# Output projection's entry: three weight tiles move from SyncE's DMA queue to ScalarE's

## The chip, the cores and the metric

The kernel runs on one core of a Trainium2 chip. A core has five engines that run their own instruction streams: TensorE (PE in the profile, with its weight loads as PEld), VectorE (DVE), ScalarE (ACT), GpSimd (POOL) and SyncE (SP). SP computes nothing here; it issues most of the DMA transfers. ACT and POOL can issue transfers too, and a transfer that ACT issues stands in ACT's instruction stream, between its activations. The metric is the device time of one execution in microseconds (us), as the median of several runs.

## The reference

One inference step of a hybrid decoder layer, in float32, for a prompt of 1024 tokens and for 8 sequences of 8 new tokens each, with a paged cache of 8192 past positions. Cut to its core:

```python
n = rmsnorm(h, g_mix);  u = n @ w_in                    # one input projection
o_gla = gated linear attention (4 heads, chunked, exact recurrence)
o_mla = latent attention (8 heads; the sampled tokens attend over the paged cache:
        per page: kv = ckv @ w_kvup, rms-normed keys, running softmax)
h = h + concat([o_gla, o_mla]) @ w_o                    # output projection, 1024 x 1024
y, conv_new = conv_ffn(rmsnorm(h, g_ffn), conv_prev)    # 1024 -> 2816 -> 1024, width-3 conv
h = h + y
h = h + (p @ ple_w_proj) * sigmoid(rmsnorm(h, g_ple) @ ple_w_gate)
```

The outputs are h for prompt and samples, the new cache rows, and the new states.

## The kernel before

Every float32 product is made of pairs: `split` (L113 to L117) casts a tile to a rounded high part on ACT (L115) and subtracts it on DVE for the low part (L116), and a product is three matmuls, high by high, high by low, low by high (L139 to L141; in the output projection L1432, L1435 and L1436).

The work has two streams. The *dense* stream is the prompt's: input projection, gated linear attention, prompt attention. The *cache* stream is the samples' attention over 64 blocks of cached pages. A cache block gathers its pages (craw and krraw, by POOL's indirect DMA), transposes them (ctp, L522), splits them (cTh, cTl), and multiplies them by the key weights (ks, L139 to L141), whose squares ACT takes (csq, L560) and DVE sums (css, L565). DVE and POOL make the norms and the scores from that (ca and cy at L588 to L590, sn at L592 and L594, the block's maximum ml at L598 and L599, which PE transposes at L616 as mt). ACT takes the exponential (L628), and PE the product with the values (cpv, L645). The rotary part of the keys goes through crp (L500), kTh and kTl, and csr.

A loop at the end of `dense` hands out cache steps by a table of due times while there is dense work. When the dense stream ends, at about 1060 us, the generator `wo_units` takes its place: units of the prompt's output projection are then placed between the remaining cache blocks. The order of the instructions on each engine is set by a scheduler, which simulates the program when it is built; on each engine they run in that order.

The output projection's inner dimension is cut into chunks of 128 rows; a group has two chunks, and a group's work has four quarters (half the prompt's tokens by half the output's columns). For a unit `wo_unit` (L1422) multiplies the two chunks' attention rows (`sh`, `sl`) by the chunks' weights (`wh`, `wl`) into one bank ps_dn, and DVE adds it to the row block of h (L1439). Four kinds of raw data come in:

- `wo_rows(c, n)` (L1403) loads 256 KB of attention output of chunk c (oraw, from a scratch in DRAM) and splits it.
- `wo_cols(c, f)` (L1413) loads 256 KB of the weight w_o of chunk c and column half f (wraw) and splits it into wdh and wdl.
- `hrows(t)` (L1550) is the tile of the prompt's rows t, eight of them of 512 KB each, into which x_prompt is loaded.
- `conv_state` (L1478) loads the convolution's weights (cvec) and state (sc), which PE transposes (pt_cv, pt_sc).

oraw, wraw, cvec and sc share one ring of three buffers (`stage`, L1395): the fourth load waits until the first buffer's subtraction is done. At the first group's first quarter the loads are issued in this order on SP: two oraw and the first wraw (these three stand early, while the dense stream still runs), four rows h0 to h3, the second chunk's wraw, row h4, the two wraw of the other column half, rows h5 to h7, and the rows of x_sample. Each DMA also has one of a few completion semaphores, which it shares with an earlier transfer, and it waits until that one has landed.

Of the kernel before, what the change touches and what calls it, by code (L numbers as in the profile page):

```python
# [18 lines left out]
P = 128  # L19
# [25 lines left out]
def step_kernel(ctx: ExitStack, tc: tile.TileContext, A):  # L45
    nc = tc.nc
    pe, act, dve, pool, sp = nc.tensor, nc.scalar, nc.vector, nc.gpsimd, nc.sync
# [1348 lines left out]
    def stage(shape, dt, name):  # L1396
        return z["sg"].tile(shape, dt, tag="stage", name=name, bufs=3)
# [7 lines left out]
    def wo_rows(c, n):  # L1405

        hl = [z["wf"].tile([P, 512], F32R, tag=f"s{n}{k}", name=f"s{k}", bufs=2) for k in "hl"]
        raw = stage([P, 512], F32, "oraw")
        sp.dma_start(raw, doT[c * P:(c + 1) * P, n * 512:n * 512 + 512])
        split(*hl, raw)  # L1410
        wos[c, n] = hl

    def wo_cols(c, f):  # L1413

        hl = [z["wq"].tile([P, 512], F32R, tag=f"wd{f}{k}", name=f"wd{k}", bufs=2) for k in "hl"]
        raw = stage([P, 512], F32, "wraw")
        sp.dma_start(raw, A["w_o"][0][c * P:(c + 1) * P, f * 512:f * 512 + 512])
        split(*hl, raw)
        wow[c, f] = hl

    def hrows(t):
        return z["hs"] if t == NT else z["h"][t] if isinstance(z["h"], dict) else z["h"][:, t, :]  # L1422
# [113 lines left out]
    def wo_units():  # L1536

        for g in range(3):  # L1540
            grp = (2 * g, 2 * g + 1)
            f0 = g % 2
            quarters = ((0, f0), (0, 1 - f0), (1, 1 - f0), (1, f0))
            for q, (n, f) in enumerate(quarters):
                if g == 0 and q == 0:
                    for ld, x in ((wo_rows, 0), (wo_cols, 0)):
                        for c in grp:
                            ld(c, x)
                    for t in range(NT):
                        sp.dma_start(hrows(t), A["x_prompt"][0, t * P:(t + 1) * P, :])  # L1550
                        if t == 3:
                            for ld, x in ((wo_cols, 1), (wo_rows, 1)):
                                for c in grp:
                                    ld(c, x)
                    sp.dma_start(z["hs"], A["x_sample"].rearrange("b t d -> (b t) d"))
                    yield
                for t in range(4 * n, 4 * n + 4):
                    wo_unit(grp, t, f)
                    if q == 2 and t == 4 and g < 2:
                        for e in range(2):  # L1560
                            down_sample([(oTg[:, c], wow[c, e]) for c in grp], pd, e)
                    yield
                nx = (grp[0] + 2, grp[1] + 2)
                for c in nx:
                    if q == 1:
                        wo_rows(c, 0)
                    elif q == 2:
                        wo_cols(c, 1 - f0)
                    elif q == 3:
                        wo_cols(c, f0)  # L1570
                        wo_rows(c, 1)
            if g == 0:
                conv_state()
                gain("g_ffn")
                sp.dma_start(z["WvT"].rearrange("p (h c) -> p h c", h=8),
                             A["mla_w_kvup"][0].rearrange("p (h c) -> p h c", c=P)[:, :, 64:128])
        for t in order:
            for f in range(2):
                wo_unit((6, 7), t, f)
                if f:  # L1580
                    normed(t)
                yield
# [103 lines left out]
    ring = [0]  # L1686
# [569 lines left out]
```

## Time and profile before

| | us |
|---|---|
| median of 3 runs | 2216.89 |
| lowest and highest run | 2215.88, 2218.55 |
| the profiled execution's own time | 2221.39 |
| its span in the profile | 2219.6 |
| mean granted TensorE clock in it | 0.984 of full speed |
| the stretch from the end of the dense stream to the last unit of the first quarter | about 1060 to 1089 |

In the rows below, L1417 is line 1417 of the kernel before; out<-in names the tiles, xcount the number of instructions, and a bracket at the end of a row is the time that the engine stood idle before it, and what ended that idle time. "SPq" and "ACTq" are the DMA issues of SP and ACT: their time is that of the issue, not of the transfer. An engine's granted clock (PEclk) is 1.00 at full speed. Rows of a timeline begin with the start in us and the length.

### The profile page before, as it was taken

Reading aid. Unit: us, or ns where it says so; the run is one execution under the profiler, and the core shown is the slowest. Engines: PE = TensorE matmul, PEld = TensorE weight load, DVE = VectorE, ACT = ScalarE, POOL = GpSimd, SP = SyncE. Lnnn points to the kernel's source line nnn. Section 1 sums busy time; section 2 is a strip of 40 time slices with the busy share of each in tenths; the row PEclk is TensorE's granted clock in tenths of the full one; section 3 lists DMA queues with packets and bytes.
Section 4 is the critical chain, followed back from the end, with each engine's and each line's share of the span. In section 5 each row is a group of like instructions: output and inputs, shape, how many; then the busy total and the mean of one; then the engine's idle time right before and its main releaser. Section 6 shows DMA issues by size and latency. Waiting matters only on the chain.

```text
span 2219.6 us, 38384 instructions
## 1 busy us (share of the span) xinstructions
PE 2134.6 (96%) x13460; PEld 1934.7 (87%) x13460; DVE 1666.6 (75%) x2551; ACT 1369.1 (62%) x3726; POOL 1227.5 (55%) x1330
## 2 busy tenths in 40 slices
PE   7999999999999999999999987999999999999999
PEld 6888978878888888887788876999999999888899
DVE  4775676467788888887888878888888886887642
ACT  5576766777778888887777766433333433534631
POOL 5675668576777777777445557666656562011100
PEclk9899999999999999999999998999999999999999
DMA  5343234412342222221521212322232325778321
GB/s 181 110 141 110 77 117 157 141 54 69 104 120 60 64 73 61 60 56 46 167 80 57 76 66 96 105 92 95 91 100 91 100 87 190 238 222 237 98 72 41
DMA packets 204418, 233.07 MB, mean 105 GB/s; under 512 B 42422, under 2 KB 146339, under 8 KB 204227
## 3 DMA queue, kind: packets, MB, share of 16 engines
q1 hardware_dynamic: 188259, 179.49, 25.8%
q0 software_dynamic: 14736, 46.67, 7.3%
q10 hardware_dynamic: 1232, 4.46, 0.5%
q8 instruction: 108, 1.77, 0.3%
q14 instruction: 83, 0.68, 0.1%
HBM read 188.00 MB, written 42.52 MB: 104 GB/s over the span
## 4 chain that ended last, share of the span: by engine, by line
PE 80%; DVE 7%; ACT 5%; DMA 4%; POOL 2%; issue 2%; SPq 0%; DVEq 0%; POOLq 0%; ACTq 0%
PE ps_gu L140 7%; PE ps_gu L141 7%; PE ps_gu L139 7%; PE ks L139 5%; PE ks L141 5%; PE ks L140 4%; PE ps_dn L141 3%; PE ps_dn L140 3%; PE ps_dn L139 3%; PE cpv L645 2%; PE ctp L522 2%; PE ps_lt L278 2%; PE ps_pj L139 2%; PE ps_pj L140 1%; PE ps_pj L141 1%
## 5 line engine op out<-in xcount | busy, mean ns | idle before, releaser
L560 ACT ACTIVATE csq<-ks 128x256 f32<-128x256 f32 x1040 | 392.2, 400 | 88.1 <-PE ks L141 78.0
L565 DVE TENSOR_REDUCE css<-csq 128x16 f32<-128x1024 f32 (+1 forms) x264 | 315.8, 1197 | 63.0 <-ACT csq L560 61.9
L115 ACT CAST wh<-st 128x512 fp32r<-128x512 f32 x176 | 108.4, 619 | 188.6 <-PE ps_gu L140 166.0
L139 PE MATMUL ks<-mv0h,cTh 128*128 128x320 f32 (+1 forms) x520 | 171.9, 333 | 6.9 <-ACT csq L560 3.0
L139 PE MATMUL ks<-mv1h,cTh 128*128 128x320 f32 (+1 forms) x520 | 170.4, 329 | 7.6 <-ACT sn L562 3.6
L604 POOL TENSOR_TENSOR chl<-craw,chl 128x1024 fp32r<-128x1024 f32 x64 | 141.8, 2216 | 57.9 <-ACT chl L603 57.2
L140 PE MATMUL ks<-mv1l,cTh 128*128 128x320 f32 (+1 forms) x520 | 154.0, 298 | 0.0
L140 PE MATMUL ks<-mv0l,cTh 128*128 128x320 f32 (+1 forms) x520 | 153.0, 296 | 0.0
L141 PE MATMUL ks<-mv0h,cTl 128*128 128x320 f32 (+1 forms) x520 | 148.6, 298 | 0.9 <-DVE cTl L116 0.8
L141 PE MATMUL ks<-mv1h,cTl 128*128 128x320 f32 (+1 forms) x520 | 148.9, 300 | 0.0
L630 POOL TENSOR_TENSOR phl<-sn,phl 128x512 fp32r<-128x512 f32 (+1 forms) x64 | 84.8, 1326 | 108.2 <-ACT phl L629 107.9
L116 DVE TENSOR_TENSOR wl<-st,wh 128x512 fp32r<-128x512 f32 x132 | 119.0, 903 | 28.5 <-ACT wh L115 28.5
L116 POOL TENSOR_TENSOR wl<-st,wh 128x512 fp32r<-128x512 f32 x44 | 69.4, 1580 | 103.5 <-ACT wh L115 98.2
L141 PE MATMUL ps_dn<-o 128*128 128x512 f32 x308 | 120.2, 390 | 0.0
L140 PE MATMUL ps_dn<-o 128*128 128x512 f32 x308 | 120.1, 390 | 0.1
L116 DVE TENSOR_TENSOR cTl<-ctp,cTh 128x512 fp32r<-128x512 f32 (+1 forms) x136 | 90.1, 663 | 39.4 <-ACT cTh L115 38.4
L139 PEld LDWEIGHTS ks<-mv0h,cTh 128*128 128x128 f32 x520 | 99.1, 191 | 20.7 <-ACT sn L562 7.1
L562 ACT COPY sn<-ks 128x64 f32<-128x64 f32 x520 | 116.8, 225 | 0.0
L139 PEld LDWEIGHTS ks<-mv1h,cTh 128*128 128x128 f32 x520 | 99.6, 191 | 19.7 <-ACT sn L562 7.4
L1317 POOL TENSOR_TENSOR pl<-p,ph 128x512 fp32r<-128x512 f32 (+1 forms) x96 | 97.1, 1016 | 31.7 <-DVE ph L1316 21.5
L139 PE MATMUL ps_dn<-o 128*128 128x512 f32 x308 | 112.1, 390 | 0.0
L139 PE MATMUL ps_gu<-xrh,wh 128*128 128x320 f32 x352 | 108.6, 309 | 1.1 <-ACT xrh L115 1.1
(672 smaller groups left out, 7875.3 us busy)
## 6 DMA issues: line engine op xcount, KB each, us to landing
raw<-ds SPq DMA_DIRECT2D x77, 256.0 KB
raw<-ffn_w_down SPq DMA_DIRECT2D x66, 256.0 KB
stage<-w_in SPq DMA_DIRECT2D x48, 256.0 KB
st<-ffn_w_gate SPq DMA_DIRECT2D x44, 256.0 KB
st<-ffn_w_up SPq DMA_DIRECT2D x44, 256.0 KB
wr<-ffn_w_down SPq DMA_DIRECT2D x44, 256.0 KB
ds<-cv SPq DMA_DIRECT2D x21, 512.0 KB
oraw<-doT SPq DMA_DIRECT2D x16, 256.0 KB
```

Of the source, the lines that this page charges most:

```text
L115: cast = act.copy(hi, src)
L116: res = (lo_eng or dve).tensor_tensor(lo, src, hi.bitcast(F32), ALU.subtract)
L139: pe.matmul(ps, ah, bh, start=first, stop=False)
L140: pe.matmul(ps, ah, bl, start=False, stop=False)
L141: return pe.matmul(ps, al, bh, start=False, stop=last)
L278: pe.matmul(ps, x, w, start=first, stop=last)
L560: act.activation(sq[:, f * 256:f * 256 + 256], ks[:, 0:256], AF.Square)
L562: act.copy(o.sn[:, g0 + i, :], ks[:, 256:320])
L565: dve.tensor_reduce(o.ss[:, g0 + i + 1 - n:g0 + i + 1, :].rearrange("p i h -> p (i h)"), sq2[:, :n].rearrange("p i (h n) -> p (i h) n", n= ...
L604: pool.tensor_tensor(ch[:, c0:c1, 128:256], src, ch[:, c0:c1, 0:128].bitcast(F32), ALU.subtract)
L630: pool.tensor_tensor(phl[:, :nt, 64:128], sb, phl[:, :nt, 0:64].bitcast(F32), ALU.subtract)
L1317: pool.tensor_tensor(pl[:, c0:], p[:, c0:], ph[:, c0:].bitcast(F32), ALU.subtract)
```

## The change

The second chunk's weight load and the two of the other column half at the entry go out through ACT's DMA queue. The first chunk's load, all rows of attention output, all rows of x_prompt and the loads of the later quarters stay on SP. The number of transfers, their sizes and the ring of three buffers are as before.

```diff
-    def wo_cols(c, f):
+    def wo_cols(c, f, ring=sp):
 
         hl = [z["wq"].tile([P, 512], F32R, tag=f"wd{f}{k}", name=f"wd{k}", bufs=2) for k in "hl"]
         raw = stage([P, 512], F32, "wraw")
-        sp.dma_start(raw, A["w_o"][0][c * P:(c + 1) * P, f * 512:f * 512 + 512])
+        ring.dma_start(raw, A["w_o"][0][c * P:(c + 1) * P, f * 512:f * 512 + 512])
         split(*hl, raw)
         wow[c, f] = hl
...
                 if g == 0 and q == 0:
-                    for ld, x in ((wo_rows, 0), (wo_cols, 0)):
-                        for c in grp:
-                            ld(c, x)
+                    for c in grp:
+                        wo_rows(c, 0)
+                    for c, ring in zip(grp, (sp, act)):
+                        wo_cols(c, 0, ring)
                     for t in range(NT):
                         sp.dma_start(hrows(t), A["x_prompt"][0, t * P:(t + 1) * P, :])
                         if t == 3:
-                            for ld, x in ((wo_cols, 1), (wo_rows, 1)):
-                                for c in grp:
-                                    ld(c, x)
+                            for c in grp:
+                                wo_cols(c, 1, act)
+                            for c in grp:
+                                wo_rows(c, 1)
```

The instruction order on the engines changes between about 1064 and 1190 us of the profile before. On ACT, at the place where the moved loads now stand (the csq and sn are a cache block's, cTh its transposed pages):

```order
 L115 CAST cTh_15065<-ctp_15060 128x512
 L560 ACTIVATE csq_15011<-ks_15029 128x256
+L1417 DMA wraw_14742<-w_o 128x512
 L588 ACTIVATE ca_15047<-cy_15046 128x64
+L1417 DMA wraw_14752<-w_o 128x512
+L1417 DMA wraw_14758<-w_o 128x512
 L560 ACTIVATE csq_15080<-ks_15081 128x256
 L562 COPY sn_14985<-ks_15081 128x64
```

The three issues stand around one activation of a cache block, ahead of its next csq. On DVE, around the subtraction wdl of the second chunk's weights (wraw_14742 is that tile; L598 is the maximum of a block's scores):

```order
 L565 TENSOR_REDUCE css_14986<-csq_15011 128x16
 L589 SCALAR_TENSOR_TENSOR ca_15047<-css_14802,ca_15047 128x64
+L590 SCALAR_TENSOR_TENSOR cy_15046<-ca_15047,cy_15046 128x64
 L565 TENSOR_REDUCE css_14986<-csq_15080 128x16
-L590 SCALAR_TENSOR_TENSOR cy_15046<-ca_15047,cy_15046 128x64
+L598 TENSOR_REDUCE ml_15055<-sn_14801 128x64
 L116 TENSOR_TENSOR wdl_14741<-wraw_14742,wdh_14740 128x512
-L598 TENSOR_REDUCE ml_15055<-sn_14801 128x64
+L622 TENSOR_SCALAR mt_15174,bm_15176<-mt_15174,bm_14965 128x128
 L1439 TENSOR_TENSOR h0_14699<-h0_14699,ps_dn_15104 128x512
 L116 TENSOR_TENSOR wdl_14751<-wraw_14752,wdh_14750 128x512
```

L590 moves ahead of a sum of squares, and L598 ahead of wdl, which stood in front of it. On PE, at the second chunk's three matmuls of the first unit:

```order
 L522 MATMUL ctp_15190<-ident_61,craw_14975 128x128 x4
 L1432 MATMUL ps_dn_15104<-wdh_14740,sh_14728 128x512
+L616 MATMUL mt_15174<-ident_61,ml_15055 128x128
 L1435 MATMUL ps_dn_15104<-wdl_14741,sh_14728 128x512
 L1436 MATMUL ps_dn_15104<-wdh_14740,sl_14729 128x512
```

The transpose of the block's maximum (L616) moves between the first two of them. And on ACT a little later, at the cast of the fourth weight tile (wraw_14758), the last of the three that moved:

```order
 L115 CAST cTh_15142<-ctp_15137 128x512
 L560 ACTIVATE csq_15112<-ks_15130 128x256
-L635 ACTIVATE mb_15184<-bm_15176,bm_14965 128x1
+L115 CAST wdh_14756<-wraw_14758 128x512
+L628 ACTIVATE sn_14801<-sn_14801 128x512
 L560 ACTIVATE csq_15161<-ks_15162 128x256
 L562 COPY sn_14985<-ks_15162 128x64
 L115 CAST cTh_15195<-ctp_15190 128x512
```

The cast and the exponential L628 move ahead of csq_15161 (the cast stood directly behind that of wraw_14752 before, and L628 came later). On SP the eight rows of x_prompt stand in a row, with no weight load between them. Beyond about 1190 us the order on PE is the same in both kernels.

## Prediction

> **What bounds the kernel now.** I read the page's busy shares and the chain that ended last, then the chain, PE's idle time and the DMA issues around the entry of the output projection (1059 to 1075 us), and last the granted clock there.
>
> ```profile
> PE 2134.6 (96%) x13460; PEld 1934.7 (87%) x13460; DVE 1666.6 (75%) x2551; ACT 1369.1 (62%) x3726; POOL 1227.5 (55%) x1330
> PE 80%; DVE 7%; ACT 5%; DMA 4%; POOL 2%; issue 2%; SPq 0%; DVEq 0%; POOLq 0%; ACTq 0%
> ```
>
> PE is the bound: busy 96% of the span and 80% of the chain. The change saves only where PE stands idle, or runs at a lower clock, because of the loads that it moves. The chain at that place:
>
> ```profile
> 1062.14 0.70 DVE sl L116
> ...
> 1062.86 5.92 DMA wraw<-w_o
> 1068.81 0.63 ACT wdh L115
> ```
>
> The second chunk's weight half-row waits for a stage buffer, which DVE frees at 1062.84 (the split of the first oraw); it leaves at 1062.86 and takes 5.92 us. Then come the cast, the subtraction and PE. PE's own rows (start, length, in brackets the idle time before):
>
> ```profile
> 1066.38 1.03 PE L522 MATMUL ctp<-ident,craw 128*128 128x128 f32 x8
> 1069.48 0.49 PE L1432 MATMUL ps_dn<-wdh,sh 128*128 128x512 f32 x1 [2.06 <-ACT wdh L115]
> 1070.82 0.71 PE L1435 MATMUL ps_dn<-wdl,sh 128*128 128x512 f32 x1 [0.85 <-DVE wdl L116]
> ```
>
> PE idles 2.06 + 0.85 = 2.91 us. Each stretch below shows its length, busy us (and instructions) of PE, PEld, DVE, ACT and POOL, PE's granted clock, the DMA share and GB/s:
>
> ```profile
> 1062.00:1069.00 7.00, 3.96 (x25) 3.08 (x23) 5.29 (x9) 4.46 (x17) 1.12 (x2) 1.00 1.02 393
> 1067.50:1070.90 3.40, 0.57 (x2) 0.27 (x2) 1.59 (x4) 1.20 (x2) 2.34 (x2) 1.00 1.03 354
> 1071.00:1074.40 3.40, 3.40 (x13) 3.17 (x14) 2.63 (x4) 2.27 (x6) 0.23 (x1) 0.51 1.03 415
> 1146.00:1149.40 3.40, 1.68 (x9) 1.17 (x9) 3.13 (x3) 1.78 (x6) 2.35 (x2) 1.00 0.37 114
> 1149.50:1156.00 6.50, 5.89 (x21) 5.20 (x21) 2.86 (x6) 2.10 (x7) 3.73 (x3) 0.50 0.62 197
> ```
>
> After the stretch in which PE worked 0.57 of 3.40 us, the clock is 0.51 for 3.4 us, which costs another 3.4 x 0.5 = 1.7 us. So the entry costs 2.91 + 1.7 = 4.6 us of 2219.6; more than that the change can win only at the later clock dip (1149.5, 6.5 us at 0.50: 3.3 us), after the waits for state_conv.
>
> **The change, part by part.** SP's issues first:
>
> ```profile
> 1059.70 1.98 SPq L1550 DMA_DIRECT2D h<-x_prompt  x4
> 1062.86 0.33 SPq L1417 DMA_DIRECT2D wraw<-w_o  x1
> 1063.24 0.43 SPq L1550 DMA_DIRECT2D h<-x_prompt  x1
> 1063.77 1.11 SPq L1417 DMA_DIRECT2D wraw<-w_o  x2
> 1064.93 2.32 SPq L1550 DMA_DIRECT2D h<-x_prompt  x3
> ```
>
> Three wraw leave SP, and five rows h4 to h7 and x_sample move up by about 1 to 3 us: h4 and h5 follow the first four at once, at 1061.7 and 1062.2; h6 and h7 still wait for h1 and h2 to land (their semaphores are shared with those). The rows are consumed far later, so this saves nothing, but it puts six rows of 512 KB, not four, into SP's queue before the weights leave. On ACT the issues stand behind one activation:
>
> ```profile
> 1064.22 0.44 ACT L560 ACTIVATE csq<-ks 128x256 f32<-128x256 f32 x1
> 1068.81 0.62 ACT L115 CAST wdh<-wraw 128x512 fp32r<-128x512 f32 x1 [2.54 <-DMA wraw<-w_o]
> 1071.95 0.62 ACT L115 CAST wdh<-wraw 128x512 fp32r<-128x512 f32 x1 [0.28 <-DMA wraw<-w_o]
> 1077.25 0.38 ACT L560 ACTIVATE csq<-ks 128x256 f32<-128x256 f32 x1 [0.33 <-DVE css L565]
> 1319.47 0.36 ACTq L1592 DMA_DIRECT2D dhp<-h  x1
> ```
>
> A. *The second chunk's load.* It goes out at about 1064.3, behind the csq at 1064.22: 1.45 us later than the 1062.86 of before, but no longer behind four rows in one queue. Where an ACT issue stands beside other work it is 0.36 us (last row). Three of them push back the csq's behind them by at most 3 x 0.36 = 1.1 us; ACT then waits 2.54 us for the weights, so that is covered. What the load takes on ACT's queue beside SP's rows no row shows. Bounds, from transfers on a third queue and from the entry itself:
>
> ```profile
> krraw<-cache_krope,idx POOLq DMA_INDIRECT x64, 2.9
> craw<-cache_ckv,idx POOLq DMA_INDIRECT x64, 4.4
> ```
>
> At the lower end 256 KB lies near the 128 KB and 512 KB of these (2.9 and 4.4 us; by size 2.9 + 1.5 x 128 / 384 = 3.4, an estimate): landing at 1067.7. At the upper end the queues act as one: then two more rows stand ahead than before, 512 KB at 393 GB/s each 1.33 us, and 1068.78 + 2 x 1.33 = 1071.45. Between them, at half of 393 GB/s, 256 KB take 0.67 us more than alone: 1067.7 + 0.67 = 1068.4. I take 1068.4, since the POOL gathers land in their medians beside SP's traffic; that is 0.4 us earlier than before.
>
> [...]
>
> What follows the load is not the load, though. In the order, DVE's L598 now stands ahead of wdl, and PE's L616 between the two matmuls. Their rows, and POOL's that L598 waits for:
>
> ```profile
> 1066.30 1.22 DVE L565 TENSOR_REDUCE css<-csq 128x16 f32<-128x1024 f32 x1
> 1067.44 0.21 DVE L590 SCALAR_TENSOR_TENSOR cy<-ca,cy 128x64 f32<-128x64 f32 x1
> 1069.46 1.31 DVE L116 TENSOR_TENSOR wdl<-wraw,wdh 128x512 fp32r<-128x512 f32 x1 [1.81 <-ACT wdh L115]
> 1070.69 1.04 DVE L598 TENSOR_REDUCE ml<-sn 128x64 f32<-128x512 f32 x1
> 1067.80 1.07 POOL L592 TENSOR_TENSOR sn<-sn,cy 128x512 f32<-128x512 f32 x1 [8.67 <-DVE cy L590]
> 1068.95 1.27 POOL L594 TENSOR_TENSOR sn<-sn,sr 128x512 f32<-128x512 f32 x1
> 1071.80 0.23 POOL L599 COPY ml<-ml 128x64 f32<-128x64 f32 x1 [1.58 <-DVE ml L598]
> L116 DVE TENSOR_TENSOR wdl<-wraw,wdh x4: 684/685/1309, 1063.4 to 1073.2; 128x512 fp32r<-128x512 f32 x4
> ```
>
> L590 takes the slot at 1066.30. L592 started 0.36 us after L590 (1067.80 - 1067.44), so now at 1066.66; L594 1.15 us later, 1067.81 to 1069.08. L598 then runs 1069.12 to 1070.16, and wdl starts as it ends, 1070.1, and takes 0.685 us (the median; the 1.31 stood beside POOL's L594, which is over by then): 1070.78, so L1435 at 1070.82. L616 fits in between: POOL's L599 runs 1070.2 to 1070.45, ahead of wdl's end. That is the 1070.82 of before: **0.0 us**, for every landing up to 1069.45 (1070.1 less the cast's 0.62 and 0.03 of gaps). L1432 starts about 0.4 us earlier, which helps nobody. PE is idle as much in sum as before, so I leave the 1.7 us of the slow clock where they are. The earlier landing is swallowed by DVE's new order, whose L598 comes 1.5 us earlier, for a softmax whose next PE instruction waited little.
>
> B. *The third and fourth tile.* They follow on ACT's queue and land 0.67 us apart, 1069.1 and 1069.8, before their casts (1071.06 and 1071.95 before), where ACT waited 0.28 us: nothing on PE, which is fed by ks then. But ACT's order now puts the third cast and L628 ahead of the csq's of 1075.66 and later:
>
> ```profile
> 1078.25 0.68 ACT L628 ACTIVATE sn<-sn 128x512 f32<-128x512 f32 x1
> 1086.04 0.39 PE L139 MATMUL ks<-mv0h,cTh 128*128 128x256 f32 x1 [0.35 <-ACT sn L562]
> 1146.29 0.39 PE L139 MATMUL csr<-qbd0h,kTh 128*128 128x256 f32 x1 [1.02 <-ACT kTh L115]
> 1149.20 0.33 PE L1494 MATMUL pt_sc<-ident,sc 128*128 128x128 f32 x1 [1.06 <-DMA sc<-state_conv]
> 1150.14 0.39 PE L1494 MATMUL pt_sc<-ident,sc 96*128 96x96 f32 x1 [0.61 <-DMA sc<-state_conv]
> ```
>
> That is 0.62 + 0.68 = 1.30 us of ACT work in front of results that PE overwrites next; ACT's 0.33 us of idle time at 1077.25 covers part, and a third of a microsecond more is saved because the bias activation L635 goes forward. Between 0 and 1.30 - 0.33 - 0.29 = 0.7 us; **+0.35**, the middle, since both ends are equally near.
>
> C. *The tail pieces around 1081 to 1087.* POOL's value product (L645), crp and csr stand earlier. The PE wait of 0.35 us at 1086.04 may go (-0.35), or a wait like csr's on kTh (1.02) may come (+1.0), because DVE's kTl now stands behind a split of oraw. I take **0**: the 0.35 us is the nearer row in place, and it may go or stay.
>
> D. *The state_conv waits.* Its loads use the same three stage buffers, and order moves its transposes little, a little ahead of csr. The two waits of 1.06 and 0.61 us may go, or as much may come: **0**, ends -1.7 and +1.7, which is also the size of one 3.4 us stretch at half clock.
>
> Sum: 0.0 + 0.35 + 0 + 0 = +0.35 us on the profiled execution of 2221.39 us (span 2219.6, the rest lies around it): 2221.7. That execution is 4.5 us above the runs' median of 2216.89, which themselves lie between 2215.88 and 2218.55. On the median it is 2216.89 + 0.35 = **2217.2 us**. About 0.2%, 4.4 us, is what a measurement of this kernel can tell from no change.
>
> **The rivals.**
>
> *The rows stay ahead (slower).* If ACT's queue gives the load no share until the rows are through, it lands at the upper end, 1071.45: 2.0 us after the point (1069.45) from which it decides. Then cast 0.62, wdl 0.685 and gaps of 0.08 put L1435 at 1072.9, 2.05 us late. PE is idle 5 us instead of 2.9, and the slow clock lasts a second stretch of 3.4 us as at 1149.5 (6.5 us): +1.7. ACT's csq's and the third cast jam behind the wait: +0.9 (the upper part of B and C). Sum +4.7: 2221.6. For it: the share of 1.02 from 1062 to 1069, and six rows ahead. Against it: craw's 4.4 us for twice the bytes.
>
> *Order jams (within 0.2%).* B, C and D at their upper ends, 0.7 + 1.0 + 1.7 = 3.4: 2220.3. Against it: the waits of this kind that the trace has between 1060 and 1160 are 1.0 us and less.
>
> *The clock doesn't fall (faster).* PE's idle time now comes as two shorter pieces with L1432 and L616 between; if the granted clock then stays at 1.00, the entry wins 1.7 us, and if the shift takes the conv dip along (6.5 x 0.5 = 3.3), 5.0: 2216.89 - 5.0 = 2211.9. Against it: PE worked 1.68 of the 3.40 us ahead of 1149.5 and the clock still fell.
>
> [...]
>
> *The load hides anyway.* That the change does nothing at the end that matters is the forecast itself: DVE's order, not the load, sets L1435.
>
> **How the numbers follow.** Forecast 0.45 (its own range 2215.0 to 2219.5: B to D at half their ends, and the half spread of the runs, 1.35), jams 0.08, clock 0.23, rows ahead 0.24. Faster by over 0.2% takes the clock case (0.23), slower the rows (0.24), the rest 0.53. The range reaches from 2211.9 - 1.35 = 2210.5 to 2221.6 + 1.35 = 2223.0.
>
> **What would show it.** Right: no wait of wdh over 2.1 us on PE, L1435 within 0.3 us of its place behind the last ctp, wdl waiting for L598 instead of the cast, PE's clock at about 0.5 for one stretch of 3.4 us. Wrong: the wraw on ACT's queue takes over 5.2 us from 1064.3 and wdl waits for the cast (rows ahead); no half clock after 1071 (clock case); new PE waits of over 1 us for csq, sn or kTh between 1075 and 1150 (jams); or a difference that arises outside 1060 to 1190 us.

## The result, and the profile after

The changed kernel is slower. Its median is 2228.55 us (six runs, 2225.39 to 2231.14) against 2218.86 us (six runs, 2215.88 to 2219.91) for the kernel before: a ratio of 1.0045, 95% interval 1.0032 to 1.0058, or +10 us. The profiled execution took 2231.14 us with a span of 2229.3 us (before: 2221.39 and 2219.6), at a mean granted clock of 0.981 (0.984).

The busy shares of the page after, first: no engine has more work to speak of, and PE has 7 us more over the same 13460 matmuls (2134.6 us before), at the lower mean clock (0.981, before 0.984).

```profile
PE 2141.6 (96%) x13460; PEld 1938.9 (87%) x13460; DVE 1669.2 (75%) x2551; ACT 1368.2 (61%) x3726; POOL 1227.7 (55%) x1330
```

The timeline after, SP's issue of the rows and ACT at the place where the loads now stand:

```profile
1058.96 7.89 SPq L1551 DMA_DIRECT2D h<-x_prompt  x8
...
1062.13 3.98 ACTq L1417 DMA_DIRECT2D wraw<-w_o  x1
...
1066.15 0.26 ACT L588 ACTIVATE ca<-cy 128x64 f32<-128x64 f32 x1 [2.24 <-issue]
1066.23 0.83 ACTq L1417 DMA_DIRECT2D wraw<-w_o  x2
...
1071.80 0.62 ACT L115 CAST wdh<-wraw 128x512 fp32r<-128x512 f32 x1 [2.72 <-DMA wraw<-w_o]
...
1074.81 0.62 ACT L115 CAST wdh<-wraw 128x512 fp32r<-128x512 f32 x1 [1.90 <-DMA wraw<-w_o]
```

The first of the three issues holds ACT's instruction stream for 3.98 us (1062.13 to 1066.11); the other two take 0.83 us together. It began as soon as DVE had freed the stage buffer (the first subtraction sl ends at 1062.09), not behind ACT's csq. ACT's activations ahead of it ran on beside it, and then ACT stood idle for 2.24 us before L588. The weights landed by 1071.78, 5.67 us after that issue had ended. What became of it on PE:

```profile
1062.82 0.42 PE L139 MATMUL ks<-mv0h,cTh 128*128 128x320 f32 x1 [1.37 <-ACT csq L560]
...
1067.65 0.58 PE L139 MATMUL ks<-mv0h,cTh 128*128 128x256 f32 x1 [2.98 <-ACT sn L562]
...
1069.32 0.63 PE L1436 MATMUL ps_dn<-wdh,sl 128*128 128x512 f32 x1
...
1072.47 0.51 PE L1432 MATMUL ps_dn<-wdh,sh 128*128 128x512 f32 x1 [1.28 <-ACT wdh L115]
...
1073.20 0.50 PE L1435 MATMUL ps_dn<-wdl,sh 128*128 128x512 f32 x1
```

A wait of 2.98 us for ACT's sn is new, and the wait for wdh is 1.28 us, not 2.06. Against the same instructions before, the two traces run apart like this: the block's ks at the entry stands 0.74 us earlier (1062.82, before 1063.56), L1436 of the first chunk 3.18 us later (before 1066.14), L1435 of the second chunk 2.38 us later (before 1070.82), and the second unit's L1432 3.0 us later. At the end of the stretch whose order changed, about 1190 us, it is 7.3 us; at the first matmul of the feed-forward part, 9.6 us (1391.2 and 1400.8); and the spans differ by 9.7. Counted from the block's ks, to which the kernel after came 0.74 us early, about 3.7 us arise at the entry, some 4.3 us more up to 1190 (the second slow stretch below, 3.4 x (1 - 0.56) = 1.5; kTl, 2.16; 0.65 at the convolution's tiles), and 2.3 us further on, where the order is the same in both.

The granted clock after (columns: length, busy us and instructions of PE, PEld, DVE, ACT, POOL, then PE's clock, DMA share, GB/s):

```profile
1066.80:1070.20 3.40, 2.55 (x9) 2.15 (x10) 1.21 (x2) 1.54 (x6) 2.35 (x2) 0.55 1.02 407
1080.40:1083.80 3.40, 3.21 (x10) 2.63 (x10) 1.78 (x3) 1.86 (x9) 1.12 (x1) 0.56 0.24 82
1320.00:1325.00 5.00, 3.46 (x11) 2.63 (x12) 2.64 (x8) 2.98 (x8) 3.66 (x5) 0.82 0.01 3
1325.00:1330.00 5.00, 5.00 (x24) 4.18 (x23) 3.51 (x5) 2.39 (x7) 2.16 (x5) 0.84 0.27 111
```

There are two stretches near half clock at the entry (0.55 and 0.56) where the kernel before had one (0.51 from 1071.0 to 1074.4), and a fall at 1320 (0.82), which the kernel before does not have at the same instructions. Ahead of that fall PE waits just as long in both kernels. Before, then after:

```profile
1314.05 0.33 PE L616 MATMUL mt<-ident,ml 128*128 128x128 f32 x1 [1.87 <-POOL ml L599]
```

```profile
1321.03 0.33 PE L616 MATMUL mt<-ident,ml 128*128 128x128 f32 x1 [1.88 <-POOL ml L599]
```

But the kernel before works on at full speed (1.00):

```profile
1315.00:1320.00 5.00, 5.00 (x24) 4.11 (x25) 3.12 (x6) 1.96 (x4) 3.81 (x4) 1.00 0.01 3
```

The last place is the tail of the second unit. DVE, POOL and PE after:

```profile
1087.45 1.44 POOL L594 TENSOR_TENSOR sn<-sn,sr 128x576 f32<-128x576 f32 x1
1087.58 4.01 DVE L116 TENSOR_TENSOR sl<-oraw,sh 128x512 fp32r<-128x512 f32 x1 [1.12 <-ACT sh L115]
1088.84 2.19 POOL L604 TENSOR_TENSOR chl<-craw,chl 128x1024 fp32r<-128x1024 f32 x1
...
1091.51 0.41 DVE L116 TENSOR_TENSOR kTl<-crp,kTh 128x256 fp32r<-128x256 f32 x1
...
1091.98 0.39 PE L141 MATMUL csr<-qbd0h,kTl 128*128 128x256 f32 x1 [2.16 <-DVE kTl L116]
```

and before:

```profile
1082.82 1.43 POOL L594 TENSOR_TENSOR sn<-sn,sr 128x576 f32<-128x576 f32 x1
1083.04 1.75 DVE L116 TENSOR_TENSOR sl<-oraw,sh 128x512 fp32r<-128x512 f32 x1
1084.74 1.01 POOL L473 DMA_INDIRECT krraw<-cache_krope,idx  x1 [0.49 <-PE crp L500]
1085.32 0.68 DVE L116 TENSOR_TENSOR sl<-oraw,sh 128x512 fp32r<-128x512 f32 x1
```

The split sl takes 0.68 us with POOL's arithmetic out of the way, 1.75 beside one POOL subtraction, and 4.01 beside two in a row; it ends 0.54 to 0.56 us after POOL's run has ended (1084.25 before, 1091.03 after). In the new order kTl stands directly behind it, and PE waits 2.16 us for kTl.

### The profile page after: what moved, and what is told of

Same layout as the page of the kernel before. It is cut to its first block, busy times and chain, and to the rows that moved or that the text cites. A ratio compares the mean times of both kernels' runs of the same rounds, so it can differ in the third digit from the quotient of the medians.

```text
span 2229.3 us, 38387 instructions
## 1 busy us (share of the span) xinstructions
PE 2141.6 (96%) x13460; PEld 1938.9 (87%) x13460; DVE 1669.2 (75%) x2551; ACT 1368.2 (61%) x3726; POOL 1227.7 (55%) x1330
## 4 chain that ended last, share of the span: by engine, by line
PE 46%; DVE 2%; ACT 2%; DMA 1%; POOL 1%; issue 1%; SPq 0%; ACTq 0%; DVEq 0%; POOLq 0%
PE ps_gu L141 7%; PE ps_gu L140 7%; PE ps_gu L139 7%; PE ps_dn L140 3%; PE ps_dn L141 3%; PE ps_dn L139 3%; PE ps_pg L141 1%; PE ps_pg L139 1%; PE ps_pg L140 1%; PE ks L139 1%; PE ps_dn L1432 1%; PE ps_dn L1435 1%; PE ps_dn L1436 1%; PE ks L140 1%; PE ks L141 1%
## 5 line engine op out<-in xcount | busy, mean ns | idle before, releaser
L604 POOL TENSOR_TENSOR chl<-craw,chl 128x1024 fp32r<-128x1024 f32 x64 | 141.4, 2209 | 57.0 <-ACT chl L603 55.2
L116 DVE TENSOR_TENSOR wl<-st,wh 128x512 fp32r<-128x512 f32 x132 | 118.9, 903 | 29.2 <-ACT wh L115 29.2
L116 POOL TENSOR_TENSOR wl<-st,wh 128x512 fp32r<-128x512 f32 x44 | 69.2, 1574 | 104.5 <-ACT wh L115 104.5
L116 DVE TENSOR_TENSOR cTl<-ctp,cTh 128x512 fp32r<-128x512 f32 (+1 forms) x136 | 89.9, 661 | 39.9 <-ACT cTh L115 38.6
```

What stands on the lines that cost most here:

```text
L116: res = (lo_eng or dve).tensor_tensor(lo, src, hi.bitcast(F32), ALU.subtract)
L604: pool.tensor_tensor(ch[:, c0:c1, 128:256], src, ch[:, c0:c1, 0:128].bitcast(F32), ALU.subtract)
```

## The experiments

Four suspects: (1) the long issue on ACT, (2) the late landing, (3) the other two loads with the order that the scheduler makes around them, and (4) the clock. Ratios are to the kernel before, run on the same chip, with the 95% interval. Two single ratios have to differ by about 0.0015 for a difference to be clear.

### Which of the three loads, and which queue

The diffs are against the kernel after.

```diff
 act_second:                    wo_cols(c, 1, act)                ->  wo_cols(c, 1)
 act_others:   for c, ring in zip(grp, (sp, act))                 ->  zip(grp, (sp, sp))
 warm:         for c, ring in zip(grp, (sp, act))                 ->  zip(grp, (act, act))
 pool_ring:    zip(grp, (sp, act)); wo_cols(c, 1, act)            ->  zip(grp, (sp, pool)); wo_cols(c, 1, pool)
```

In "warm" the first chunk's load goes out through ACT too. It stands at 646 us, long before the rows.

> Only the second chunk's load goes out on ACT's queue; the two of the other column half stay on SP. Queue theory (ACT's issue of its first load holds ACT up for about 4 us, because the transfer queues are busy or because it is the queue's first transfer): ACT's issue again takes about 4 us from 1062, PE again waits about 3 us for sn, and the time is 5 to 9 us above the kernel before. Order theory (the loss comes from the new order of DVE and ACT, with L598 ahead of wdl, the third cast and kTl late): DVE's order here has wdl ahead of L598 as in the kernel before, so no more than 2 us above it.

> Only the two loads of the other column half go out on ACT's queue; the second chunk's stays on SP behind four rows. PE's order is that of the changed kernel, instruction for instruction. Queue theory: the first of the two issues takes about 4 us from 1063, PE waits about 3 us for sn, 5 to 9 us above the kernel before; if the stall falls where ACT waits for the weights anyway, 3 to 6. Order theory: as slow as the changed kernel, 9 to 10 us above the kernel before, with no long issue on ACT.

> As the changed kernel, and the first chunk's load (some 400 us earlier) goes out on ACT's queue too, so that the entry's load isn't the queue's first. First-use theory: the entry's issue falls from 4.0 to about 0.4 us, the long issue shows at about 650 us instead, and the time falls by 3 to 6 us against the changed kernel. Load theory (SP's rows in flight hold the issue up): the entry's issue stays at about 4 us, and the time at the changed kernel's, within 2 us.

> As the changed kernel, but the three loads go out on POOL's queue, where POOL has idle time at 1060 to 1067. Queue theory: no stall of ACT or PE at 1064 to 1067; what is left is the landing of the weights behind or beside the rows, 0 to 5 us above the kernel before. Order theory (POOL's kernel has an order near the changed one's): 8 to 10 us above the kernel before.

| kernel | median, us | ratio |
|---|---|---|
| act_second | 2224.74 | 1.0032 (1.0020 to 1.0044) |
| act_others | 2228.44 | 1.0043 (1.0029 to 1.0057) |
| warm | 2225.45 | 1.0029 (1.0019 to 1.0039) |
| pool_ring | 2223.17 | 1.0016 (1.0007 to 1.0025) |

The first ACT issue is long in both halves of the change. act_second, then act_others:

```profile
1060.66 3.78 ACTq L1417 DMA_DIRECT2D wraw<-w_o  x1
```

```profile
1060.90 3.11 ACTq L1417 DMA_DIRECT2D wraw<-w_o  x1
...
1064.10 0.39 ACTq L1417 DMA_DIRECT2D wraw<-w_o  x1
```

and short in warm, where ACT's queue had carried a transfer before:

```profile
646.30 0.40 ACTq L1417 DMA_DIRECT2D wraw<-w_o  x1
...
1059.42 0.34 ACTq L1417 DMA_DIRECT2D wraw<-w_o  x1
...
1060.02 0.33 ACTq L1417 DMA_DIRECT2D wraw<-w_o  x1
...
1060.74 0.33 ACTq L1417 DMA_DIRECT2D wraw<-w_o  x1
```

So the length belongs to the queue's first transfer at this place, not to every issue beside the rows. Without it ACT's L588 does not wait for an issue and PE's wait of 2.98 us for sn is gone, but the time comes down only from 1.0045 to 1.0029. In act_others the second chunk's load is back on SP and PE's order is that of after. By the medians it costs about as much as the whole change. But its trace has no wait for wdh at the entry, and L1435 comes 8.5 us after the block's ks, against 10.4 us in after and 7.3 us before, and the comparison by stretches further down has 3.6 us between the two, so the late second chunk is not shown to be free. act_second is the cleanest of the four: on PE, ACT, DVE and POOL its order is that of the kernel before from end to end, by the lines and tiles in the profile. One tile on the other queue gives 1.0032 with no new order at all. On POOL's queue there is no block on ACT, but in the order made for it PE waits 4.15 us for POOL's ml in one piece, and it is still slower than before.

### The first transfer, the rows behind it, and the stage buffers

warm_slpool and warm_second start from warm, rows_late from after, stage5 from the kernel before:

```diff
 warm_slpool:  split(*hl, raw)  ->  split(*hl, raw, pool)     (the second half's two oraw: sl on POOL)
 warm_second:  wo_cols(c, 1, act)  ->  wo_cols(c, 1)          (first and second chunk on ACT only)
 rows_late:    rows h2 to h7 written behind the first units, two at a time
 stage5:       stage ring bufs=3  ->  bufs=5
```

> As warm, and the two subtractions sl of the second half's oraw run on POOL instead of DVE; PE's order differs from warm's in 22 rows. Order theory (DVE's sl stands ahead of kTl and takes 4.4 us, because it runs beside two POOL operations in a row; csr waits for kTl): the PE wait of 2.6 us for kTl is gone, sl on POOL takes 1.5 to 2.5 us behind L604, and the time is 2.5 to 5 us below warm. Rival (PE would have waited there for something else, or the loss sits in the clock): within 1.5 us of warm.

> As the changed kernel, with only h0 and h1 issued at the entry and the other six rows after the first three units; ACT's queue carries nothing before the entry. If the long issue needs both a first transfer and busy transfer queues: at 1062 two rows at most are in flight, and the issue takes under 1.5 us, no wait of PE for sn over 1 us. If a first transfer at this place is long by itself: about 4 us again. The weights land by 3 to 4 us after their issue; the time lies between the kernel before and 4 us above it, or below the kernel before if the landing at 1065 to 1066 spares the wait for wdh and the half clock (up to 4 us).

> The first chunk's load (early) and the second's go out on ACT's queue, the two others on SP: act_second with an earlier first transfer. First-use theory: issue of 0.4 us instead of 3.8, 2 to 5 us below act_second; since the order on DVE has wdl ahead of L598 and kTl not behind a long sl, within 3 us of the kernel before. The load shares the transfer engines with four or five rows and lands no earlier than in the kernel before (5.9 us after its issue), so no gain over 2 us against it.

> The kernel before with five stage buffers instead of three, all loads on SP: the second chunk's and one of the other half's weights are loaded long before the entry. Theory (the entry costs 2.9 us of waiting and 1.7 us of half clock because a load waits for a buffer): the waits of ps_dn for wdh and wdl are gone and PE's clock stays at 1.0 after 1071: 3 to 5 us below the kernel before. Rival (the order that the scheduler then sets brings another wait, like kTl's): between 2 below and 5 above.

| kernel | median, us | ratio |
|---|---|---|
| warm_slpool | 2229.60 | 1.0042 (1.0029 to 1.0055) |
| rows_late | 2227.26 | 1.0034 (1.0022 to 1.0046) |
| warm_second | 2222.66 | 1.0014 (1.0005 to 1.0022) |
| stage5 | 2222.58 | 1.0014 (1.0005 to 1.0023) |

With warm_second four kernels make a table:

| | first ACT transfer at the entry | first one at 646 us |
|---|---|---|
| all three loads on ACT | 1.0045 | 1.0029 |
| only the second chunk's | 1.0032 | 1.0014 |

Its columns differ by 0.0016 and 0.0018 (3.5 and 4.0 us): the long issue. Its rows differ by 0.0013 and 0.0015 (2.9 and 3.3 us): the other two loads, with the order that goes with them. What is left, 1.0014 (0.0005 to 0.0022, about 3 us), is neither. From the intervals, the mean of each pair is uncertain by about 0.0011 (2.4 us), and the order is not held fixed (act_second has that of the kernel before, the others have their own), so these are sizes and not exact shares. The traces, compared by stretches further down, give other sizes.

rows_late told little of what it was made for: the scheduler put the late rows back, and SP issued all of them from 1058.05 on, with x_sample among them, so the loads met the same queue, and the issue took 4.60 us. stage5 gives the weights their buffers early. PE's waits for wdh and wdl at the entry are gone, and PE waits elsewhere (2.44 us for sn at 1071.53). The kernel is not faster, but that says little about the entry itself: its order differs from far ahead of the entry, its trace, counted by matmuls started, is 8.4 us behind that of before when it comes there, and by the L616 that the kernel before has at 1208.78 it has made up 4.6 us of them. SP's queue has a long issue in it too:

```profile
1081.11 3.96 SPq L1417 DMA_DIRECT2D wraw<-w_o  x1
```

and in the kernel before:

```profile
1071.10 2.87 SPq L1409 DMA_DIRECT2D oraw<-doT  x1
```

That queue had carried hundreds of transfers by then (299 issues ahead of 1071 us in the kernel before). So a first transfer is one way to a long issue, and not the only one.

warm_slpool went against its purpose. DVE and POOL in it:

```profile
1085.05 0.43 DVE L116 TENSOR_TENSOR kTl<-crp,kTh 128x256 fp32r<-128x256 f32 x1 [1.39 <-ACT kTh L115]
1085.08 1.45 POOL L594 TENSOR_TENSOR sn<-sn,sr 128x576 f32<-128x576 f32 x1
1085.48 5.96 DVE L668 TENSOR_TENSOR acclo<-pvs,acclo 64x258 f32<-64x258 f32 x1
1086.47 2.21 POOL L604 TENSOR_TENSOR chl<-craw,chl 128x1024 fp32r<-128x1024 f32 x1
1088.63 2.53 POOL L116 TENSOR_TENSOR sl<-oraw,sh 128x512 fp32r<-128x512 f32 x2
...
1094.06 0.39 PE L139 MATMUL ks<-mv0h,cTh 128*128 128x256 f32 x1 [3.15 <-ACT sn L562]
```

kTl is early now, but the next DVE operation with two inputs in on-chip memory and neither of them a matmul's bank, L668 (0.41 us in the kernel after), took 5.96 us: it stood beside four POOL operations in a row and ended 0.28 us after the last. What sl met, L668 met in its place. As sl did with its 4.01 us, it ended only after the whole of POOL's run, and not between two of its operations. cTl (L116), which reads a matmul's bank (ctp), shows no such length: in the kernel before it took 0.68 us at 1085.92 beside POOL's L604 (1085.76 to 1088.05), and 0.69 us at most in all 136, while L596 (sn from sn and nmask, neither of them a bank) took 1.23 us at 1086.91 beside the same L604, ended 0.09 us after it, and takes 0.22 us in the median. What in the hardware holds DVE up, no run shows.

### Taking single costs out

warm_chl starts from warm and moves one subtraction (L604, of block 48) from POOL to DVE; hs_act starts from after and sends x_sample first on ACT's queue; act_rows8 is the kernel before with the eight rows of x_prompt on ACT (the weights stay on SP); stage4 is the kernel before with four stage buffers.

```diff
-                pool.tensor_tensor(ch[:, c0:c1, 128:256], src, ...
+                (dve if o.n == 48 and c0 == 0 else pool).tensor_tensor(ch[:, c0:c1, 128:256], src, ...
...
+                    act.dma_start(z["hs"], A["x_sample"].rearrange("b t d -> (b t) d"))
...
-                        sp.dma_start(hrows(t), A["x_prompt"][0, t * P:(t + 1) * P, :])
+                        act.dma_start(hrows(t), A["x_prompt"][0, t * P:(t + 1) * P, :])
```

> As warm, and one subtraction of one cache block (L604 of the block at 1083, 128x1024) runs on DVE instead of POOL, so that POOL has only L594 beside DVE's sl; PE's order is warm's but for one row. Port theory (a DVE subtraction with both inputs in on-chip memory ends only its own length after POOL's run of operations has ended): sl takes no longer than 2.0 us instead of 4.4, kTl follows at once, PE's wait for kTl falls from 2.6 to under 1.5 us, 1 to 3 us below warm. Rival (sl waits for its input, a late oraw): sl stays at 4 us or more, no gain.

> The kernel before with all eight rows of x_prompt on ACT's queue and all weights on SP. The first row is the first transfer of ACT's queue, at the same place in the program as the changed kernel's load, but SP's queue carries no rows. If the long issue needs a backlog on SP's queue: the first row's issue takes under 0.7 us. If a first transfer at this place is long by itself: 3 to 5 us. The time itself says little, since ACT then waits for h1 and h2 to land before the rows that share their semaphores: 2 to 15 us above the kernel before.

> As the changed kernel, and x_sample's rows (256 KB) go out on ACT's queue shortly ahead of the three weight loads, with SP's rows already under way. Theory (the first transfer on ACT's queue pays, whatever it carries, when SP's queue has a backlog): x_sample's issue takes 3 to 4.6 us and the three weight loads 0.33 to 0.4 us each; the time is within 3 us of the changed kernel's. Rival (it is the weight load that is slow, for the buffer it waits for): x_sample 0.5 us, the weight load 4 us.

> The kernel before with four stage buffers instead of three, all loads on SP: the second chunk's weights are loaded long before the entry, the other half's two still wait for a buffer. Theory (the entry's 2.9 us of waiting and 1.7 us of half clock come from that one load): PE doesn't wait for wdh or wdl of the second chunk; 2 to 5 us below the kernel before. Rival (as in stage5, the scheduler's new order brings other waits of the same size): 0 to 5 us above.

| kernel | median, us | ratio |
|---|---|---|
| warm_chl | 2224.63 | 1.0026 (1.0015 to 1.0036) |
| act_rows8 | 2230.65 (one run) | |
| hs_act | 2229.46 | 1.0054 (1.0041 to 1.0067) |
| stage4 | 2226.65 | 1.0031 (1.0019 to 1.0043) |

In warm, sl took 4.42 us and PE waited 2.58 us for kTl. In warm_chl:

```profile
1087.22 1.93 DVE L116 TENSOR_TENSOR sl<-oraw,sh 128x512 fp32r<-128x512 f32 x1
...
1089.53 0.38 PE L141 MATMUL csr<-qbd0h,kTl 128*128 128x256 f32 x1 [0.71 <-DVE kTl L116]
```

The mechanism is shown: one POOL operation less in the row makes sl 2.5 us shorter and the wait 1.9 us shorter. A gain in the time is not shown: 1.0026 against 1.0029, two medians that can't tell 2 us apart.

hs_act has a short first transfer (0.58 us, 1.4 us after SP had begun to issue the rows), and has the highest ratio of all:

```profile
1060.04 0.58 ACTq L1546 DMA_DIRECT2D hs<-x_sample  x1
...
1062.10 0.36 ACTq L1417 DMA_DIRECT2D wraw<-w_o  x1
...
1067.49 0.82 ACTq L1417 DMA_DIRECT2D wraw<-w_o  x2
1068.37 0.26 ACT L588 ACTIVATE ca<-cy 128x64 f32<-128x64 f32 x1 [4.49 <-DMA hs<-x_sample]
```

The second weight load waited for x_sample's to land (it shares its completion semaphore), the third stands behind it, and ACT waited with them: 4.49 us. So the same block came back by another way. In act_rows8, where SP's queue has no rows, the first row's issue took 0.40 us at 1057.01; from the fourth row's issue to the end of the last, ACT's stream was held for 12.39 us, its waits for earlier rows to land included. stage4's entry lost its waits for wdh and wdl as in stage5, and got a wait of 1.74 us for csq; its trace, too, is late at the entry (9.2 us) and makes up 4.9 us by 1208.78.

### The long issue once more, POOL's queue, and both kernels again

tiny sends 256 bytes on ACT's queue at the start of the output projection, ahead of everything else there; pool_second is after with the second chunk's load on POOL and the other two on SP. before_again and after_again are the two kernels unchanged.

```diff
+        act.dma_start(z["WvT"][0:1, 0:64], A["mla_w_kvup"][0][0:1, 0:64])
...
-                    for c, ring in zip(grp, (sp, act)):
+                    for c, ring in zip(grp, (sp, pool)):
-                                wo_cols(c, 1, act)
+                                wo_cols(c, 1)
```

> As the changed kernel, and one load of 256 bytes on ACT's queue at about 1060, ten instructions ahead of the weight loads; nothing else moves. First-use theory (a queue's first transfer is issued slowly once SP's rows fill the transfer engines; before that, and later, it is quick): the small load's issue 0.4 to 0.6 us, the weight loads 0.33 to 0.4 us each, the time as warm's, 2 to 5 us below the changed kernel. Rival (what made warm quick was the other place of the first weight tile): the first weight load still takes about 4 us, the time within 2 us of the changed kernel's.

> Only the second chunk's load goes out on POOL's queue, the two others on SP: act_second without any issue on ACT. If ACT's issue is what costs: no stall of ACT, 2 to 5 us below act_second (that is 1 to 5 above the kernel before). A gain against the kernel before only if the load lands by 1067 in spite of the rows and the clock doesn't fall at the entry: 1 to 4 below.

> The kernel before once more, for its clock at the projection's end (1295 to 1385). If the rest of the loss, 3 us that warm_second has in a stretch with the same order, belongs to the kernel: again about 10 us lost to the half clock there, no dip at 1310 to 1325. If it belongs to the execution: another sum, 8 to 14 us, with the dips in other places.

> The changed kernel once more: the first issue on ACT again 3 to 4.6 us, sl again about 4 us beside POOL's L594 and L604, PE's waits for sn and kTl as before. At the projection's end, if the loss there belongs to the kernel: again about 13.5 us lost to the half clock between 1295 and 1385; if to the execution, another sum.

| kernel | median, us | ratio |
|---|---|---|
| tiny | 2229.88 | 1.0049 (1.0035 to 1.0062) |
| pool_second | 2224.03 | 1.0025 (1.0015 to 1.0035) |
| before_again | 2218.29 (one run) | |
| after_again | 2231.36 (one run) | |

In tiny the small transfer took 0.52 us to issue, the first weight load 0.37:

```profile
1063.90 0.52 ACTq L1535 DMA_DIRECT2D WvT<-mla_w_kvup  x1
...
1065.92 0.37 ACTq L1417 DMA_DIRECT2D wraw<-w_o  x1
...
1068.06 0.82 ACTq L1417 DMA_DIRECT2D wraw<-w_o  x2
```

That agrees with a price of the first transfer, but, as in hs_act, the median is no lower for it: the second and third load go out 2.1 us behind the first (0.6 in warm), and PE waits 1.65 us for sn and 1.90 us for ml in place of 2.98. pool_second has no issue on ACT and the 4.14 us wait for ml of pool_ring; it is 1.6 us below act_second, less than the 2 to 5 that were expected and within the noise.

The pair of repeats has the entry's mechanism again: 3.78 us for the first ACT issue in after_again (1061.27), sl 4.42 us and a wait of 2.58 us for kTl. The clock after the waits at 1311 and 1321 us is again 1.00 in before_again, and 0.74 and 0.58 over two stretches of 5 us in after_again. The loss at half clock from 1295 to 1385 us (the sum over slices of 5 us of 5 x (1 - PEclk)) is 10.3 and 8.6 us in the two profiles of before, 13.65 us in both of after, 13.6 in warm_second, and 8.6 in pool_ring. That is about 4 us between the two kernels in a part whose order is the same, and warm_second, with 13.6, is the corner of the table that has only the 3 us left over. But the sum does not rank the kernels: it is 15.3 to 15.4 in warm, act_second and act_others, and 8.6 in hs_act, which is the slowest.

The traces can be laid side by side by stretches. The table has, for single profiled executions, how much longer than in the trace of before it takes from the block's ks at the entry (1063.56 before) to a later block's transpose L616 (1208.78), and from there to the first matmul of the feed-forward part (1391.17). Ahead of the entry the order is the same but for some 20 us around 650 us in the warm kernels, and yet these traces come to the entry -3.5 to +2.9 us from that of before, a scatter that every whole time contains; behind 1391.17 they differ by less than 1 us.

| trace | entry to 1208.78, us | 1208.78 to 1391.17, us |
|---|---|---|
| before_again | +0.2 | -1.5 |
| after, after_again | +8.0, +8.1 | +2.4, +3.5 |
| warm | +5.2 | +4.7 |
| warm_chl | +3.0 | +3.3 |
| act_second | +1.8 | +3.5 |
| warm_second | -0.1 | +3.0 |
| act_others | +4.4 | +3.5 |
| tiny | +2.0 | +4.0 |
| hs_act | +4.3 | +2.8 |
| pool_ring | +4.8 | -0.7 |
| pool_second | +3.0 | +3.4 |

The first column is the change itself: 8 us, in both pairs of profiles. Against it the long issue comes to 2.8 us (after and warm) and 1.9 us (act_second and warm_second), the other two loads with their order to 6.2 and 5.3 us, more than the medians' 3 us, and most of the wait for kTl to 2.2 us (warm and warm_chl). The 3 us of warm_second lie wholly in the second column, where every kernel with a changed entry but pool_ring loses 2.4 to 4.7 us. act_second does so too, with the order of the kernel before throughout. (In tiny and hs_act the order differs to about 1360.) That this part is the clock fits most of its sums, hs_act's least; why the clock falls there, and not in the kernel before and pool_ring, is open, and no run takes the fall out. tiny and hs_act are shorter than after in the first column and not by their medians; where they lose it is not known.

## Why the prediction was wrong

**Forecast.** 2217.2 us with no change was the forecast; +10 us came, above the range.

**Step A, the issue.** "Where an ACT issue stands beside other work it is 0.36 us", and three of them "covered" by ACT's wait for the weights: this is the step that failed. The row behind it (1319.47) is from a place where the DMA engines were empty (share 0.00 from 1319 to 1320 us). The first issue took 3.98 us. It is also not covered: the wait that was to cover it (2.54 us, for wdh) comes later on ACT than the csq's and L588 that the issue holds up, and those feed PE. It was not behind the csq at 1064.3 either, but at 1062.13. The medians' table prices it at about 3.5 to 4 us of the 10, the traces at 1.9 to 2.8; no run shows the whole time fall by that with nothing else changed. In the traces the larger part, 5.3 to 6.2 us, is the other two loads with the order around them, which step B and C had at +0.35 us.

**Step A, the landing.** 1068.4 was taken and 1071.78 measured, beyond the upper end of 1071.45. The upper end was met by its number and not by its working (two more rows ahead at 393 GB/s, 2.67 us). Counted from the block's ks, the tile landed 9.0 us behind it in after and 5.2 us before. In warm the same six rows stand ahead and the issue is short, and it landed after 6.0 us: 0.8 us later than before. By this comparison the other 3 us of the lateness are the long issue; that they brought it to the upper end is chance. DMA queues after, from 1066 to 1068 us (q1 is SP's, q10 ACT's; packets, MB, share of the 16 engines):

```profile
q1 hardware_dynamic: 225, 0.83, 104.0%
```

and from 1070 to 1074 us:

```profile
q1 hardware_dynamic: 233, 0.81, 59.2%
q10 hardware_dynamic: 289, 0.53, 44.8%
```

ACT's queue moves nothing for 3 us after its issue (its first packet starts at 1069.20), and then has 44.8% beside SP's 59.2%, with packets of 1.8 KB in the mean (0.53 MB in 289) against 3.5 KB of SP's. In warm, with a short issue at 1059.42, the load took 6.7 us (landing 1066.1), in warm_second 6.6 us, and on POOL's queue in pool_ring 6.0 to 7.8 us, all longer than the 5.92 us on SP's queue before: where the landing can be read, the other queue did not bring it earlier.

**Step A, DVE's order.** The forecast had L598 from 1069.12 to 1070.16 and wdl behind it. DVE after:

```profile
1066.70 0.23 DVE L590 SCALAR_TENSOR_TENSOR cy<-ca,cy 128x64 f32<-128x64 f32 x1
...
1069.12 1.22 DVE L565 TENSOR_REDUCE css<-csq 128x16 f32<-128x1024 f32 x1 [2.19 <-ACT csq L560]
1070.26 1.02 DVE L598 TENSOR_REDUCE ml<-sn 128x64 f32<-128x512 f32 x1
1072.45 0.69 DVE L116 TENSOR_TENSOR wdl<-wraw,wdh 128x512 fp32r<-128x512 f32 x1 [1.18 <-ACT wdh L115]
```

L590 was 0.40 us late (forecast 1066.30). The sum of squares css, ahead of L598 in the order, waited 2.19 us for ACT's csq, so L598 ended at 1071.28. Even without the late weights wdl would have started 1.2 us after the forecast's 1070.1; with them it started at 1072.45. "L1432 starts about 0.4 us earlier" became 3 us later (1072.47 and 1069.48).

**Step B.** The third and fourth tile did not land at 1069.1 and 1069.8: ACT waited another 1.90 us for the third at 1074.81. Of +0.35, upper end 0.7, the sign was right. The 3 us of the medians, and 5.3 to 6.2 us of the traces, for the other two loads are larger, but they hold step C and the second slow stretch too.

**Step C.** Taken 0, upper end +1.0. It names the very place, "DVE's kTl now stands behind a split of oraw", and prices it by csr's wait on kTh (1.02). The wait is 2.16 us (2.58 in warm and after_again), because the split grew to 4.01 us beside two POOL operations in a row. The prediction had a row for this effect (wdl 1.31 us beside L594, 0.685 alone) and used it for wdl only. In warm_chl's trace, without most of it, the stretch is 2.2 us shorter than in warm's, which is about what the wait lost; the medians do not resolve it.

**Step D.** The waits for the convolution's tiles are 1.81 us (cvec) and 0.88 us (sc) after, and were 0.37 us (cvec) and 1.06 + 0.61 us (sc) before: +0.65 us, inside the ends.

**The rivals.** "The rows stay ahead" came nearest: the landing was 2.3 us behind the point from which it decides (1071.78 and 1069.45). But most of that lateness came from the issue and not from the rows, and ACT's queue did get a share (10.8% from 1066 to 1070 us, beside 91.5% of SP's) before the rows were through. Its 2221.6 us fell short by 7 us, since it has no block of ACT, no split of 4 us, and one more stretch of slow clock, where there is another one 240 us later. "Order jams" had places right and ends too small: they were taken from the waits that the kernel before happened to have. "The clock doesn't fall" was wrong: it fell twice at the entry (0.55 and 0.56), where it had fallen once (0.51).

**The clock.** "I leave the 1.7 us of the slow clock where they are" counted only the entry. A wait of 1.87 us left the clock at 1.00 in the kernel before, and after one of 1.88 us it was 0.82 and 0.84 over two stretches of 5 us in the kernel after: the length of the wait alone does not decide. What does, no run here shows, and the fall can't be forecast by these rows.

## What to carry to other kernels

ACT's first DMA through its own queue, put behind the backlog of SP's, took 3.1 to 4.6 us to issue in five profiles, and ACT's arithmetic stood idle for 2.0 to 3.8 us of it (after_again, act_second, after, rows_late). Look for a row in the same state of load before pricing an issue at 0.36 us, and ask what stands behind it on the issuing engine. Moving a load to another queue did not bring it in earlier while the DMA engines were full (share 1.02 in the kernel before and after): 6.0 to 7.8 us in warm, warm_second and pool_ring, and 5.92 on SP's queue before. A difference of a few us in the whole time is best looked for by stretches between the same instructions, since the rest of the execution differs by as much. Price every reordering by who works beside whom: a subtraction of 0.68 us became one of 4 us because two operations on POOL had moved together.

## What the runs showed of the hardware

- The first transfer through ACT's queue behind SP's rows took 3.1 to 4.6 us to issue (3.98, 3.78, 3.11, 4.60, 3.78 in five profiles); once the queue had carried a transfer, 0.33 to 0.40 us beside the same rows. In four of the five it ended 6.9 to 7.2 us after the first row's issue (7.8 in rows_late), and the one that began 0.6 us later (act_others) was the shortest: it looks like a wait for a point in the backlog rather than a fixed price. Where it came 1.4 us after the first of the rows it was short (0.58 in hs_act, 0.52 in tiny; 3.2 us after them in the changed kernel), and in tiny the next transfer, 2 us later, was short as well (0.37). Busy DMA engines alone don't make it long: in warm the first transfer at 646.30 took 0.40 us at a DMA share of 1.14. Issues of 2.87 us (before) and 3.96 us (stage5) stand on SP's queue as well. What inside the queue takes the time is open.
- DVE's subtraction sl, with neither input from a matmul's bank, took 0.68 us alone, 1.75 and 1.93 beside one POOL operation (before, warm_chl), 4.01 to 4.42 beside two that follow one another (after, after_again, warm, act_others), and L668 5.96 in place of 0.41 beside four (warm_slpool). Each of those beside POOL ended 0.28 to 0.56 us after the last of its operations.
- A transfer that waited for an earlier one to land, with which it shares a completion semaphore, held ACT by itself: 4.49 us in hs_act, with no long issue (0.58, 0.36 and 0.82 us for two).
- Early weights (stage4, stage5) remove the entry's waits and the kernel is 0.14 to 0.31% slower: with an order made anew by the scheduler, one wait less was not time won. Their traces lose ahead of the entry (8.4 and 9.2 us) and behind 1208.78 (2.9 and 4.6 us) what they win between (4.6 and 4.9 us).
